# Windowed attention beside dense projections: queries written in place, first token group first, three output tiles moved between later query projections

## The chip, the cores and the metric

The kernel runs on one core of a Trainium2 chip. The metric is device time in microseconds for one execution, as the median of several. One further execution is profiled, and everything read from "the profile" or "the trace" is of that execution. TensorE (PE) multiplies matrices, VectorE (DVE), ScalarE (ACT) and GpSimd (POOL) do elementwise work, and SyncE (SP) issues most of the DMAs. Each engine works through its own instructions in the order in which they were written; an instruction that waits holds up everything behind it on that engine.

## The reference: what is computed

Two transformer-like layers run on 1024 prompt tokens and 32 sample tokens (1056 together), model width 1024. Layer 0 mixes with a matrix-memory recurrence (mLSTM), layer 1 with attention over a window. Each layer ends in a SwiGLU feed-forward part, and each of the four sub-layers is followed by a layer norm over `alpha * x + sublayer(x)`.

The change lies in the attention of layer 1, which the reference computes so:

```
q = x @ w_q                      # 16 query heads of 64
k, v                             # 2 key/value heads of 64, shared by 8 query heads each
s = q k^T / sqrt(64) - slope * |distance|      # own chunk of 64 and the two before it: 192 keys
p = exp(s - max(s, sink)); p = p / (sum(p) + exp(sink - max))
out = (p @ v) @ w_out
x = layer_norm(alpha * x + out)
```

## The kernel before

**Tiling.** Activations lie transposed: 128 features on the partitions, tokens along the free dimension, 8 feature blocks. Tokens are cut in three groups `GRP` of 384, 384 and 288 for projections, and in four quarters of 264 for output projections. Every matrix product is done with each operand split into a high part (rounded to the 32-bit format that TensorE takes at speed) and a low rest: three matmuls per step of 128 rows (`gemm`, lines 404 to 406). A weight unit is 128 x 1024; it is loaded by SP (line 165), and each of its two halves is split by an ACT cast (line 239) and a POOL or DVE subtraction (line 241).

**Order.** The order of instructions on each engine is fixed when the kernel is built. `Weave` interleaves the work: tasks are generators that emit some instructions and then yield a number of "due" microseconds. Each step of `gemm` lets `3 * (max(n, 256) / 2400 + 0.003)` due microseconds pass, where n is the width of the moving operand, and the tasks that have come due emit their instructions there. `wv.drain` emits a task to its end, or up to a condition, without any dense step between. Weight splits are fed in the same way, one half for each 1.7 due microseconds (`FEED_W`), with at most five halves live at a time (`SLOTS`) unless a half has a tile of its own (`W.home`).

**Attention.** `attention` runs 72 items: eight query tiles j (two heads each) times nine blocks of 128 tokens (the ninth holds the 32 sample tokens); b = 0, 1, 2 belong to token group 0, b = 3, 4, 5 to group 1, b = 6, 7, 8 to group 2. An item passes `scores` (matmuls into the PSUM tile `psS`, then a DVE operation that adds the bias and takes the minimum of the negated scores), `soft` (exponential on ACT, reciprocal on DVE, scaling on POOL at lines 1829 and 1833), `turn` (transposes on PE at line 1854, split by ACT and DVE at lines 1858 and 1859), `values` (matmuls, line 1883) and `place` (ACT copy and two DVE additions into the activations, lines 1896 and 1900). Between the stages lies `gap` = `GAP_A` = 0.5: three gaps for an item, 1.5 due microseconds. The list `JG` gives the order of (pair `jp` of query tiles, token group), six items each: (0,0) (1,0) (0,1) (0,2) (1,1) (1,2), then (2,0) to (2,2), then (3,0) to (3,2).

**Queries.** `q_group(j, g)` projects the 128 query features j (two heads) for token group g. The score matmul wants the high part and the low part of one head stacked on the 128 partitions, for two heads in turn. So the result is scaled and split into the tiles `qh` (ACT, line 1659) and `ql` (DVE, line 1660), of which there is one buffer each, and then SP copies halves of 64 partitions into the tile `Q` with DMAs (line 1672): 4 for a group of 384 tokens, 8 for the group of 288, since its last chunk has 32 tokens. `q_made` counts a query tile as ready 4.0 due microseconds later. A query projection is only begun when the attention has scored all but the last group's items before it (`while ast["scored"] < 6 * (i // 2 - 1)`); until then due time passes with no dense work.

**Values, bias, ends.** `VZ` are two tiles of values with one half of the partitions zero; `pad_values` (line 1749) fills them by SP DMAs, three blocks at a time for the first key/value head, all eight at once for the second. `load_bias` loads one of four bias tiles through SP and writes its end columns on POOL (line 1697); three buffers. For b = 0 `scores` first clears one column of `psS` on DVE (line 1797).

**After the attention.** `mixed_parts` splits the mixed activations into operands for the output projection (lines 434 and 435) and reloads the residual. `mixer_out` then runs eight output tiles for each quarter of the tokens; the first quarter starts when token group 0 is placed for all heads, and the rest of the attention is woven into it. Weight units stand in the order in which they are used: twelve loads of `wqb`, then twice eight of `wout_b`.

Of the kernel before, what the change touches and what calls it, by code (L numbers as in the profile page):

```python
# [9 lines left out]
F32 = mybir.dt.float32  # L10
# [19 lines left out]
LC = 64  # L30
WK = 3 * LC
D_FF = 2816
FT = D_FF // P

# [12 lines left out]
GAP_M = (0.6, 1.666, 1.519, 1.5)  # L47
GAP_A = 0.5

# [235 lines left out]
def kernel(ctx: ExitStack, tc: tile.TileContext, A, O):  # L285
# [61 lines left out]

    U_KV, U_QB = [], []
    for _ in range(2):
        U_KV.append([add("wkv", u) for u in range(2)])  # L350
        U_QB.append([add("wqb", u) for u in range(4)])
    U_QB[1] += [add("wqb", u) for u in range(4, 8)]
    U_QB[0] += U_QB[1][4:]
    U_OUT_B = [[add("wout_b", u) for u in range(8)] for _ in range(2)]
    add_ffn(1)
# [876 lines left out]

    def mixer_out(us, li, lx, opening=None, before=None):

        box = [lx]

        def run(g, cols, after):
            if before:
                before(g)
            if g == 3:  # L1240
                lx = box[0]
                lx.sums = ExitStack()
                su = lx.sums.enter_context(pool("sums"))
                bufs = [new(su, f"su{i}", [P, 2, N4])[:] for i in range(2)]
                wv.drain(lx.norms[1])
# [3 lines left out]
            for i, m in enumerate(order):  # L1249
                u = us[g > 0][m]  # L1250
                W.get(u)
                if g < 2:
                    W.split_to(us[g][min(m + 2, KT - 1)])
                ps = psbank()[:, :N4]
                gemm(ps, wcols(u), [(SX[:, 0, k, cols], SX[:, 1, k, cols]) for k in range(KT)])
                z = ACT[:, m, cols]
                nc.vector.scalar_tensor_tensor(z, z, ALPHA, ps, op0=ALU.mult, op1=ALU.add)
# [394 lines left out]
    def q_group(j, g):  # L1652

        t0, n = GRP[g]
        ps = project(U_QB[g > 0][j], g)
        q = Q[j, g] = new(pb, "Q", [P, 2 * 384], F32R, bufs=4)
        h, l = (new(pb, tag, [P, 384], F32R)[:, :n] for tag in ("qh", "ql"))
        sc = -(HD ** -0.5)
        nc.scalar.activation(h, ps, AF.Copy, scale=sc)
        nc.vector.scalar_tensor_tensor(l, ps, sc, h.bitcast(F32), op0=ALU.mult, op1=ALU.subtract)  # L1660

        def place():
            yield 1.0
            for i in range(2):
                own, other = slice(64 * i, 64 * i + 64), slice(64 - 64 * i, 128 - 64 * i)
                for t, src in ((own, h), (other, l)):
                    for a, m in ((0, LC * (n // LC)), (LC * (n // LC), n % LC)):
                        if m:
                            w = min(m, LC)
                            d = q[t, 2 * a : 2 * a + 2 * m].rearrange("p (c h w) -> p c h w", h=2, w=w)  # L1670
                            r = src[own, a : a + m].rearrange("p (c w) -> p c w", w=w)
                            nc.sync.dma_start(d[:, :, i].bitcast(F32), r.bitcast(F32))

        return wv.launch(place())

# [32 lines left out]
    load_bias(1)  # L1708
    load_bias(2)
    load_sample_bias(0)  # L1710
# [11 lines left out]
    for j in range(4):  # L1722
        placing = q_group(j, 0)
        W.done(U_QB[0][j])
# [18 lines left out]

    def pad_values(tiles, g2):

        for i in range(2):
            r = slice(64 * i, 64 * i + 64)
            v = VR[r, tiles, g2].rearrange("p t a d -> p t (a d)")
            nc.sync.dma_start(VZ[i][r, tiles].bitcast(F32), v.bitcast(F32))

    def v_turn(group, pause):
        yield pause
        for c, c0, L, g, off in CH:
            if g == group:
                pt = new(psb, "T", [P, 512], bufs=2)
                nc.tensor.transpose(pt[:L, :P], vT[g][:, off : off + L], ident[:])
                v_parts(c, pt[:L, :P], L)
                if c % 3 == 2:
                    pad_values(slice(c - 2, min(c + 1, 8)), 0)
                ast["v"] = c + 1  # L1760
                yield 0.8

    ast = {"ready": 0, "scored": 0, "placed": 0, "v": 0}
# [8 lines left out]
    def attention(gap):  # L1772
        S, pairs_ = {}, {}

        def parts(b):

            if b == 0:
                return [(0, 130, 64, 0, 1 + P), (1, 258, P, 0, 1 + LC)]
            if b == 8:
                return [(0, 2, P + DEC, SEQ, 1)]  # L1780
            k0 = (b - 1) * P
            return [(0, 2, WK, k0, 1), (1, 2 + WK, WK, k0 + LC, 1)]

        def scores(j, b):
            _, t0, R, g, off = CH[b]
            jp = j // 2
            if (j, b) == (4, 0):
                load_bias(3)
            s = S[j, b] = {}
# [5 lines left out]
            rows = 2 * n  # L1795
            if b == 0:
                nc.vector.memset(ps[:, 194:195], 0.0)
            for c, at, nk, k0, _ in parts(b):
                lhs = q[:, 2 * (off + n * c) : 2 * (off + n * c) + rows]
                for i, k in enumerate((KH[g2], KL[g2])):  # L1800
                    nc.tensor.matmul(ps[:rows, at : at + nk], lhs, k[:, k0 : k0 + nk], start=i == 0, stop=i == 1)  # L1801
            for c, at, nk, _, w in parts(b):
                first = b != 0 and c == 0
                cols = slice(at - first, at + nk + (not first))
                bc = slice(w - first, w + nk + (not first))
                nc.vector.tensor_tensor_reduce(
                    p[:rows, cols], ps[:rows, cols], bias[:rows, j % 2, bc], 1.0, 3e38,
                    op0=ALU.add, op1=ALU.min, accum_out=st[:rows, 0, c : c + 1],
                )
# [4 lines left out]
        def soft(j, b):  # L1814
            s = S[j, b]
            p, st = s["p"], s["st"]
            rows = 2 * DEC if b == 8 else P
            for c, at, nk, _, _ in parts(b):
                first = b != 0 and c == 0
                cols = slice(at - first, at + nk + (not first))  # L1820
                nc.scalar.activation(
                    p[:rows, cols], p[:rows, cols], AF.Exp, bias=st[:rows, 0, c : c + 1], scale=-1.0,
                    accum_out=st[:rows, 1, c : c + 1],
                )
# [5 lines left out]
            else:  # L1830
                for c, at, nk, _, _ in parts(b):
                    w = p[:rows, at : at + nk]
                    nc.gpsimd.tensor_scalar_mul(w, w, st[:rows, 2, c : c + 1])
# [27 lines left out]
        def values(j, b):  # L1861
# [22 lines left out]
            if (j, b) == (3, 7):  # L1884
                pad_values(slice(0, 8), 1)

        def place(j, b):
            _, t0, R, g, off = CH[b]
            ast["placed"] += 1
            if j % 2 == 0:  # L1890
                return
            po = pairs_.pop((j // 2, b))["po"]
            n, nc_ = (DEC, 1) if b == 8 else (LC, 2)
# [23 lines left out]
    for t in spread:  # L1917
        wv.drain(t)
    wv.drain(placing)
    wv.launch(v_turn(0, 0))  # L1920
# [13 lines left out]
    def q_made():  # L1934
        yield 4.0
        ast["ready"] += 1

    for i, (j, g) in enumerate(QG):
        if i < 4:
            continue  # L1940

        while ast["scored"] < 6 * (i // 2 - 1):
            wv.tick(0.25)
        q_group(j, g)
        wv.launch(q_made())
        if g == 2:
            W.done(U_QB[1][j])
        if (j, g) == (7, 0):
            nparts[0] = 0
# [7 lines left out]
            )  # L1957

    def before(g):
        if g == 0:  # L1960
            wv.drain(task, lambda: ast["placed"] >= last_item(7, 0))
        if g < 3:
            parts_made(g)

# [4 lines left out]

    tasks, lx = mixer_out(U_OUT_B, 2, None, finish, before)  # L1970
    ffn(1, 3, tasks, lx, True)
# [132 lines left out]
```

## Time and profile before

| what | value |
|---|---|
| median of 3 runs | 2243.89 us (2242.85 to 2245.75) |
| the profiled execution's own time | 2245.04 us |
| its span, first to last instruction | 2243.3 us |
| PE busy | 2181.9 us (97%) |
| DVE, ACT, POOL busy | 1428.2, 989.4, 933.0 us (64%, 44%, 42%) |
| mean granted TensorE clock | 0.988 |
| PE busy outside 1190 to 1453 us | 1960.1 of 1980.3 us |
| PE busy from 1190 to 1453 us | 221.7 of 263.0 us |

Each line of a timeline names the start, the duration, the engine, the line of the kernel, the operation, what it writes and reads and, in brackets, how long the engine stood idle before it and what ended that. A line of waits gives total, number and longest. The attention begins at about 1216 us with the first score matmuls and its last value matmuls end at about 1453 us. Times that the prediction is made against are those of the profiled execution, 1.15 us above the median.

### The profile page before, as it was taken

What the parts mean: (1) busy time and instruction counts of PE and PEld (TensorE: products, weight loads), DVE (VectorE), ACT (ScalarE), POOL (GpSimd) and SP (SyncE); (2) the same over time, 40 slices, a digit from 0 to 9 for tenths busy, and PEclk for the clock granted to TensorE, in tenths of its full rate; (3) what the DMA queues carried; (4) which work ended last, traced back from release to release, by engine and by line L of the source; (5) the groups of instructions that cost most, each with busy time, mean ns of one, the idle gap of its engine ahead of it and who ended that gap; (6) DMA issues with size and microseconds to landing.
All of it is one profiled execution on the core that took longest, in us unless ns stands there. A gap on an engine that the chain in (4) does not pass through costs nothing.

```text
span 2243.3 us, 43908 instructions
## 1 busy us (share of the span) xinstructions
PE 2181.9 (97%) x16982; PEld 2150.6 (96%) x16982; DVE 1428.2 (64%) x2778; ACT 989.4 (44%) x2215; POOL 933.0 (42%) x920
## 2 busy tenths in 40 slices
PE   9999999999999999999997898899999999999997
PEld 9999999999999999999996888899999999999997
DVE  4465677787756565566575556688766665466657
ACT  4444455364444444322254556756444444431225
POOL 2544210005656555554444433500565556554541
PEclk9999999999999999999998999999999999999999
DMA  5222213213434433996425332421343344398722
GB/s 168 77 61 56 58 38 106 68 38 99 162 134 154 147 141 116 323 303 206 139 86 135 87 78 70 150 87 41 104 173 141 140 151 146 120 339 273 232 67 78
DMA packets 203296, 296.60 MB, mean 132 GB/s; under 512 B 53264, under 2 KB 159560, under 8 KB 203088
## 3 DMA queue, kind: packets, MB, share of 16 engines
q1 hardware_dynamic: 198736, 289.47, 39.5%
q10 hardware_dynamic: 4352, 4.33, 0.6%
q8 instruction: 134, 2.20, 0.4%
q14 instruction: 74, 0.61, 0.1%
HBM read 199.27 MB, written 82.94 MB: 126 GB/s over the span
## 4 chain that ended last, share of the span: by engine, by line
PE 85%; DVE 5%; ACT 3%; DMA 3%; issue 1%; POOL 1%; SPq 1%; ACTq 0%; POOLq 0%; DVEq 0%
PE d L404 10%; PE d L406 10%; PE d L405 10%; PE A L404 9%; PE A L406 9%; PE A L405 9%; PE B L404 7%; PE B L405 7%; PE B L406 7%; PE O L1883 1%; PE psS L1801 1%; PE T L1854 1%; ACT act L507 1%; POOL wl L241 1%; DMA hs_x<-z 1%
## 5 line engine op out<-in xcount | busy, mean ns | idle before, releaser
L241 POOL TENSOR_TENSOR wl_s<-wr,wh_s 128x512 fp32r<-128x512 f32 x224 | 304.3, 1367 | 237.1 <-ACT wh_s L239 163.7
L404 PE MATMUL d<-sx,wh 128*128 128x264 f32 (+2 forms) x1080 | 349.4, 324 | 1.4 <-ACT wh L239 1.3
L406 PE MATMUL d<-sx,wl 128*128 128x264 f32 (+2 forms) x1080 | 331.5, 307 | 2.1 <-POOL wl L241 2.1
L405 PE MATMUL d<-sx,wh 128*128 128x264 f32 (+2 forms) x1080 | 331.6, 307 | 0.2 <-DVE sx L435 0.2
L241 POOL TENSOR_TENSOR wl_a<-wr,wh_a 128x512 fp32r<-128x512 f32 x112 | 153.3, 1371 | 410.7 <-ACT wh_a L239 405.4
L404 PE MATMUL A<-sx,wh_s 128*128 128x264 f32 x896 | 254.4, 284 | 0.0
L405 PE MATMUL A<-sx,wh_s 128*128 128x264 f32 x896 | 254.2, 284 | 0.0
L406 PE MATMUL A<-sx,wl_s 128*128 128x264 f32 x896 | 254.0, 283 | 0.0
L239 ACT CAST wh_s<-wr 128x512 fp32r<-128x512 f32 x224 | 135.7, 618 | 192.3 <-DVE wr L194 102.6
L404 PEld LDWEIGHTS d<-sx,wh 128*128 128x128 f32 x1080 | 206.8, 192 | 5.8 <-ACT wh L239 2.5
L406 PEld LDWEIGHTS d<-sx,wl 128*128 128x128 f32 x1080 | 205.8, 191 | 3.5 <-POOL wl L241 3.2
L405 PEld LDWEIGHTS d<-sx,wh 128*128 128x128 f32 x1080 | 206.9, 192 | 1.8 <-DVE sx L435 0.8
L404 PE MATMUL d<-sx,ex 128*128 128x264 f32 x624 | 180.5, 289 | 0.1
L405 PE MATMUL d<-sx,ex 128*128 128x264 f32 x624 | 177.2, 284 | 0.0
L406 PE MATMUL d<-sx,ex 128*128 128x264 f32 x624 | 176.9, 284 | 0.0
L406 PEld LDWEIGHTS A<-sx,wl_s 128*128 128x128 f32 x896 | 168.8, 188 | 0.0
L405 PEld LDWEIGHTS A<-sx,wh_s 128*128 128x128 f32 x896 | 168.4, 188 | 0.0
L404 PEld LDWEIGHTS A<-sx,wh_s 128*128 128x128 f32 x896 | 168.4, 188 | 0.0
L241 POOL TENSOR_TENSOR wl<-wr,wh 128x512 fp32r<-128x512 f32 (+2 forms) x82 | 106.5, 1304 | 119.1 <-ACT wh L239 109.2
L1325 POOL TENSOR_TENSOR z<-z 128x528 fp32r<-128x528 f32 x76 | 103.4, 1360 | 126.0 <-ACT z L1324 117.1
L404 PE MATMUL A<-ex,wh_s 128*128 128x264 f32 x448 | 127.5, 285 | 0.0
L405 PE MATMUL A<-ex,wh_s 128*128 128x264 f32 x448 | 127.1, 284 | 0.0
(359 smaller groups left out, 7107.0 us busy)
## 6 DMA issues: line engine op xcount, KB each, us to landing
wr<-in_gu SPq DMA_DIRECT2D x92, 512.0 KB, 4.7
hs_x<-z SPq DMA_DIRECT2D x72, 528.0 KB, 3.0
hs_t<-z SPq DMA_DIRECT2D x64, 528.0 KB, 2.9
sx<-hs_x SPq DMA_DIRECT2D x112, 264.0 KB, 5.9
sx<-hs_t SPq DMA_DIRECT2D x64, 264.0 KB, 6.0
ex<-hs_t SPq DMA_DIRECT2D x64, 264.0 KB, 5.9
wr<-in_dn SPq DMA_DIRECT2D x32, 512.0 KB
ex<-hs_x SPq DMA_DIRECT2D x32, 264.0 KB, 5.9
```

Source lines behind the costliest of these rows:

```text
L239: self.nc.scalar.copy(hi, r)
L241: eng.tensor_sub(lo, r, hi.bitcast(F32))
L404: nc.tensor.matmul(out, ah, bh, start=start and k == 0, stop=False, **kw)
L405: nc.tensor.matmul(out, ah, bl, start=False, stop=False, **kw)
L406: nc.tensor.matmul(out, al, bh, start=False, stop=stop and k == last, **kw)
L507: nc.scalar.activation(z, z, AF.Identity, scale=gk, bias=bk)
L1325: eng.tensor_sub(lo.bitcast(F32R), buf(s), hi)
L1801: nc.tensor.matmul(ps[:rows, at : at + nk], lhs, k[:, k0 : k0 + nk], start=i == 0, stop=i == 1)
L1854: nc.tensor.transpose(pt[:nk, t, :rows], p[:rows, at : at + nk], ident[:rows, :rows])
L1883: nc.tensor.matmul(out, v[:nk], x, start=i == 0, stop=i == len(todo) - 1)
```

## The change

- **Queries in place.** `q_group` no longer makes `qh` and `ql` or any DMA. For each of the two heads, ACT writes the scaled high part from PSUM straight into its half of the partitions of `Q`, and DVE writes the low part into the other half. A group of 384 takes two ACT and two DVE instructions of 64 partitions, the group of 288 four of each (256 columns and 32 columns). `q_made` waits 2.5 instead of 4.0 due microseconds.
- **Order.** `JG` becomes (0,0) (1,0) (2,0) (3,0), then for each jp (jp,1) (jp,2). The queries of group 0 get weight loads of their own, so `wqb` is loaded 16 times instead of 12.
- **Output tiles.** After (0,2), (1,2) and (2,2) one output tile of the first quarter is computed (`EARLY` = 3); `mixer_out` skips these three. The second halves of the first quarter's output weights get one tile of their own (`home`), shared by all eight units.
- **Values and ends.** `pad_values` becomes a POOL copy of one block (64 x 128), 28 of them in all. The score layout for b = 0 moves to columns whose end is cleared once, so the clearing in `scores` goes.
- **Bias.** With the new order the four bias tiles are gone through twice; the next is loaded at each visit.
- **Pace.** `GAP_A` goes from 0.5 to 0.46.

```
-GAP_A = 0.5
+GAP_A = 0.46
...
+    for b in (0, 4):
         U_KV.append([add("wkv", u) for u in range(2)])
-        U_QB.append([add("wqb", u) for u in range(4)])
...
+        U_QB[0] += [add("wqb", u) for u in range(b, b + 4)]
+    for jp in range(QH // 4):
+        U_QB[1] += [add("wqb", 2 * jp + i) for i in range(2)]
+        if jp < EARLY:
+            U_OUT_B[0].append(add("wout_b", jp))
...
-        h, l = (new(pb, tag, [P, 384], F32R)[:, :n] for tag in ("qh", "ql"))
...
-        nc.scalar.activation(h, ps, AF.Copy, scale=sc)
-        nc.vector.scalar_tensor_tensor(l, ps, sc, h.bitcast(F32), op0=ALU.mult, op1=ALU.subtract)
...
+        for a, w in ((0, LC), (LC * (n // LC), n % LC)):
+            m = n // LC * LC if w == LC else w
+            if not m:
+                continue
+            src = ps[:, a : a + m].rearrange("p (c w) -> p c w", w=w)
+            dst = q[:, 2 * a : 2 * a + 2 * m].rearrange("p (c h w) -> p c h w", h=2, w=w)
             for i in range(2):
                 own, other = slice(64 * i, 64 * i + 64), slice(64 - 64 * i, 128 - 64 * i)
...
-                            nc.sync.dma_start(d[:, :, i].bitcast(F32), r.bitcast(F32))
...
+                h = dst[own, :, i]
+                nc.scalar.activation(h, src[own], AF.Copy, scale=sc)
+                nc.vector.scalar_tensor_tensor(
+                    dst[other, :, i], src[own], sc, h.bitcast(F32), op0=ALU.mult, op1=ALU.subtract
+                )
...
-    ENDS = (1, 2 * WK + 2)
+    ENDS = (1, 2 * WK + 2, 464)
...
+    home = [new(pb2, "oh", [P, D // 2], F32R, bufs=2)[:] for _ in range(2)]
+    W.home.update({(u, 1): home for u in U_OUT_B[0]})
...
+    def pad_values(i, c, g2):
+
+        r = slice(64 * i, 64 * i + 64)
+        nc.gpsimd.tensor_copy(VZ[i][r, c], VR[r, c, g2].rearrange("p a d -> p (a d)").bitcast(F32))
...
-    JG = [(0, 0), (1, 0), (0, 1), (0, 2), (1, 1), (1, 2)]
-    JG += [(2, 0), (2, 1), (2, 2), (3, 0), (3, 1), (3, 2)]
+    JG = [(jp, 0) for jp in range(4)] + [(jp, g) for jp in range(4) for g in (1, 2)]
...
-            if (j, b) == (4, 0):
-                load_bias(3)
+            if j % 2 == 0 and b in (0, 3):
+                ast["visit"] += 1
+                if ast["visit"] < 7:
+                    load_bias((ast["visit"] + 1) % 4)
...
-            if b == 0:
-                nc.vector.memset(ps[:, 194:195], 0.0)
...
-        yield 4.0
+        yield 2.5
...
+        while ast["scored"] < 6 * (n - 1):
             wv.tick(0.25)
-        q_group(j, g)
...
+        for j in (2 * jp, 2 * jp + 1):
+            q_group(j, g)
+            wv.launch(q_made())
+            if g != 1:
+                W.done(U_QB[g > 0][j])
...
+        if g == 2 and jp < EARLY:
+            before(0)
+            out_tile(U_OUT_B[0][jp], jp, QUARTERS[0][0])
+            W.done(U_OUT_B[0][jp])
```

More of the change, by code (lines that the diff above doesn't have):

```diff
@@ L31 @@
 WK = 3 * LC
+EARLY = 3
 D_FF = 2816
@@ L1231, with out_tile, mixer_out @@
     W.pause = FEED_W
-    def mixer_out(us, li, lx, opening=None, before=None):
+    def out_tile(u, m, cols):
+        ps = psbank()[:, :N4]
+        gemm(ps, wcols(u), [(SX[:, 0, k, cols], SX[:, 1, k, cols]) for k in range(KT)])
+        z = ACT[:, m, cols]
+        nc.vector.scalar_tensor_tensor(z, z, ALPHA, ps, op0=ALU.mult, op1=ALU.add)
+    def mixer_out(us, li, lx, opening=None, before=None, made=0):
         box = [lx]
@@ L1249, in run @@
             for i, m in enumerate(order):
+                if not g and m < made:
+                    continue
                 u = us[g > 0][m]
@@ L1253, in run @@
                     W.split_to(us[g][min(m + 2, KT - 1)])
[L1254 to L1257, printed above, removed]
+                out_tile(u, m, cols)
                 if g == 3 or u not in us[1]:
@@ L1801, in scores @@
                     nc.tensor.matmul(ps[:rows, at : at + nk], lhs, k[:, k0 : k0 + nk], start=i == 0, stop=i == 1)
[L1802 removed]
+            for c, src, at, nk, _, w in parts(b):
                 first = b != 0 and c == 0
                 cols = slice(at - first, at + nk + (not first))
+                sc = slice(src - first, src + nk + (not first))
                 bc = slice(w - first, w + nk + (not first))
                 nc.vector.tensor_tensor_reduce(
[L1807 removed]
+                    p[:rows, cols], ps[:rows, sc], bias[:rows, j % 2, bc], 1.0, 3e38,
                     op0=ALU.add, op1=ALU.min, accum_out=st[:rows, 0, c : c + 1],
@@ L1817, in soft @@
             rows = 2 * DEC if b == 8 else P
-            for c, at, nk, _, _ in parts(b):
+            for c, _, at, nk, _, _ in parts(b):
                 first = b != 0 and c == 0
@@ L1830, in soft @@
             else:
-                for c, at, nk, _, _ in parts(b):
+                for c, _, at, nk, _, _ in parts(b):
                     w = p[:rows, at : at + nk]
@@ L1891, in place @@
                 return
+            if j == 3 and 0 < b < 8:
+                for i in range(2):
+                    pad_values(i, b - i, 1)
             po = pairs_.pop((j // 2, b))["po"]
```

66 lines of the change are left out of this document (22 added, 44 removed).

## The prediction

> **What bounds the kernel now.** I read the sums by stretch first. The columns are the stretch, its length, then busy time and count of PE, PE's weight load, DVE, ACT and POOL, the granted TensorE clock, the DMA share and GB/s.
>
> ```profile
> span 2243.3 us, 43908 instructions
> ...
> 0.00:1190.00 1190.00, 1183.55 (x9175) 1170.12 (x9176) 755.86 (x1470) 508.43 (x1137) 479.47 (x533) 1.00 0.39 128
> 1190.00:1453.00 263.00, 221.73 (x1466) 207.01 (x1465) 151.69 (x590) 157.67 (x500) 114.05 (x131) 0.92 0.36 97
> 1453.00:2243.30 790.30, 776.58 (x6346) 773.44 (x6344) 520.62 (x719) 323.26 (x579) 339.50 (x257) 1.00 0.44 150
> ...
> 1190.00:1200.00 10.00, 7.33 (x31) 5.66 (x30) 8.43 (x12) 5.75 (x11) 5.36 (x4) 0.83 0.66 185
> ...
> 1210.00:1220.00 10.00, 7.89 (x30) 7.26 (x31) 2.58 (x18) 2.50 (x10) 3.46 (x4) 0.67 0.65 163
> 1220.00:1230.00 10.00, 10.00 (x55) 9.43 (x54) 4.64 (x23) 5.48 (x23) 3.16 (x5) 0.74 0.05 11
> ...
> 1270.00:1280.00 10.00, 5.93 (x26) 5.76 (x26) 5.41 (x23) 6.89 (x21) 4.95 (x5) 0.66 0.33 86
> ...
> 1360.00:1370.00 10.00, 6.50 (x31) 6.28 (x32) 5.73 (x23) 7.50 (x24) 4.91 (x5) 0.66 0.28 78
> ...
> 1453.00:1464.00 11.00, 11.00 (x93) 11.00 (x92) 7.83 (x17) 6.01 (x12) 1.29 (x1) 1.00 0.67 204
> ```
>
> Outside the attention PE idles 20 us in 1980. In the attention it idles 41.3 of 263 us, and the clock is 0.92 instead of 1. All that the change can win is there: 41.3 us, and at most 221.73 x 0.08 = 17.7 us of clock, together 59. Next, what PE waited for in that stretch (total, times, longest), and the four long waits in the timeline.
>
> ```profile
> PE T L1854 <- POOL s L1829: 15.7, 7, 5.3
> PE T L1756 <- DVE VR L1686: 9.7, 1, 9.7
> PE psS L1801 <- DVE psS L1797: 7.3, 8, 1.3
> ...
> PE psS L1801 <- DMA Q<-ql: 1.1, 2, 0.8
> ```
>
> ```profile
> 1210.50 0.47 PE L1756 MATMUL T<-ident,act 128*128 128x128 f32 x1 [9.67 <-DVE VR L1686]
> ...
> 1274.07 0.90 PE L1854 MATMUL T<-ident,s 128*128 128x128 f32 x3 [5.30 <-POOL s L1829]
> ...
> 1310.60 0.90 PE L1854 MATMUL T<-ident,s 128*128 128x128 f32 x3 [3.68 <-POOL s L1829]
> ...
> 1363.51 0.90 PE L1854 MATMUL T<-ident,s 128*128 128x128 f32 x3 [4.75 <-POOL s L1829]
> ```
>
> DVE and POOL are named, but they were themselves late. The last view, ACT's timeline just ahead of each, and the queries' tile among SP's issues, show why.
>
> ```profile
> 1200.70 0.49 ACT L1659 ACTIVATE qh<-d 128x384 fp32r<-128x384 f32 x1 [2.19 <-DMA Q<-qh]
> 1201.09 1.13 ACT L239 CAST wh<-wr 128x512 fp32r<-128x512 f32 x2
> ...
> 1208.76 0.49 ACT L1659 ACTIVATE qh<-d 128x384 fp32r<-128x384 f32 x1 [6.54 <-DMA Q<-qh]
> ...
> 1270.97 0.41 ACT L1659 ACTIVATE qh<-d 128x288 fp32r<-128x288 f32 x1 [4.17 <-DMA Q<-qh]
> ...
> 1307.65 0.41 ACT L1659 ACTIVATE qh<-d 128x288 fp32r<-128x288 f32 x1 [1.98 <-DMA Q<-qh]
> ...
> 1360.60 0.41 ACT L1659 ACTIVATE qh<-d 128x288 fp32r<-128x288 f32 x1 [4.46 <-DMA Q<-qh]
> ```
>
> ```profile
> L1672 SPq DMA_DIRECT2D Q<-qh x64: 590/605/1699, 1185.0 to 1426.0; - x64
> ```
>
> There is one `qh`. ACT can't write the next until SP's copies of the last have been read; they are 64 from `qh` and as many from `ql`, at 0.6 us of SP each, so a pair of 288-token projections takes 16 x 0.6 = 9.6 us of SP. Behind the blocked ACT instruction stand the exponentials, so POOL's scaling and PE's transposes are late too. So the long waits come from SP's copies, not from the attention's own arithmetic.
>
> **The change part by part.** *The queries' DMAs go.* The three later waits, 5.30 + 3.68 + 4.75 = 13.7 us, each fall in a g = 2 group, where two projections pass 2 x 8 x 0.369 = 5.9 due us and six items need 9.0, so that nothing dense was left to cover. With ACT free the transposes would still wait for their chain; but (0,2), (1,2) and (2,2) are exactly where an output tile now stands, 24 matmuls at 11.00 / 93 = 0.118 us = 2.8 us. I take all 13.7. At 1200 ACT would go on 2.19 us earlier, less 0.49 for the second query instruction: the casts of row 1201.09 come 1.7 us earlier, then POOL's subtraction and the third value transpose, about 1202.5 in place of 1210.5. Of 9.67 I take 7.8. The 1.1 us on `Q<-ql` goes. Sum 22.6.
>
> *The clearing of psS goes.* The 7.3 us are eight waits for a 0.06 us memset behind DVE's queue. The scores then wait for the bias operation two items earlier, still on DVE. Bounds 0 and 7.3; I take 6, since that operation stands further ahead in the queue.
>
> *The clock.* Work lost to it is busy time x (1 - clock): 7.33 x 0.17 + 7.89 x 0.33 + 10.00 x 0.26 = 6.4 us at 1190 to 1230, 5.93 x 0.34 = 2.0 at 1270, 6.50 x 0.34 = 2.2 at 1360: 10.6 next to three of the stalls. Bounds 0 and 17.7 (all of it); I take 9.
>
> *What queries in place add.* Rows by shape, with count, busy time, mean ns, idle before:
>
> ```profile
> L1660 DVE SCALAR_TENSOR_TENSOR ql<-d,qh 128x384 fp32r<-128x384 f32 x15 | 8.3, 554 | 11.7 <-ACT qh L1659 9.1 <-ACT wh L239 2.6
> L1660 DVE SCALAR_TENSOR_TENSOR ql<-d,qh 128x288 fp32r<-128x288 f32 x8 | 3.7, 458 | 20.7 <-ACT s L1821 8.7 <-DMA Q<-ql 6.8 <-ACT hi L1858 2.9
> ...
> L1900 DVE TENSOR_TENSOR act<-O,t 64x256 f32<-64x256 f32 x64 | 26.6, 415 | 5.7 <-ACT t L1896 4.5 <-PE psS L1801 0.4
> ...
> L1618 DVE TENSOR_TENSOR KL<-d,KH 128x256 fp32r<-128x256 f32 x1 | 0.4, 415 | 0.0
> ...
> L1618 DVE TENSOR_TENSOR KL<-d,KH 128x32 fp32r<-128x32 f32 x1 | 0.2, 192 | 0.3 <-ACT KH L1617 0.3
> ```
>
> ```profile
> L1659 ACT ACTIVATE qh<-d 128x384 fp32r<-128x384 f32 x15 | 7.3, 487 | 12.7 <-DMA Q<-qh 10.7 <-PE d L406 1.9
> L1659 ACT ACTIVATE qh<-d 128x288 fp32r<-128x288 f32 x8 | 3.3, 412 | 18.3 <-DMA Q<-qh 13.1 <-PE T L1854 3.2 <-PE d L406 2.0
> ...
> L1617 ACT CAST KH<-d 128x256 fp32r<-128x256 f32 x1 | 0.4, 377 | 0.0
> ...
> L1617 ACT CAST KH<-d 128x32 fp32r<-128x32 f32 x1 | 0.2, 186 | 0.7 <-DVE KL L1618 0.7
> ```
>
> Half the partitions don't halve the time (64x256 at line 1900 takes 415 ns, as 128x256 at line 1618 does). So a 384 group adds one more instruction to each engine, 0.49 and 0.55 us. The 288 group becomes two of 256 and two of 32: ACT 2 x (0.377 + 0.186) - 0.412 = 0.71, DVE 2 x (0.415 + 0.192) - 0.458 = 0.76. Over 16 and 8 groups ACT gains 13.5 us and DVE 14.9. With the eight casts of the four more weights (0.6 us each, by row 1201.09) ACT then has 158 + 18 and DVE 152 + 15 us in a stage of some 235, where PE has 263 - 41.3 - 17.7 = 204 of full-speed work: PE's matmuls hide both. Without that cover all 33 us would be on the path (0 to 33). The short waits of today (15.7 less 13.7 us on POOL's scaling) say that the queues are seldom late; I charge 3.
>
> The page "VectorE: DVE Perf Modes" of the Trainium skill, section "Two Vector instructions with no wait between them", speaks against this part: an instruction whose input or output starts in another quarter of the partitions than its predecessor's starts only when all earlier ones have finished, and the new low parts read one half and write the other. Line 1900, which also writes both halves in turn, shows no longer duration for it. What a held start can cost is the overlap of neighbours:
>
> ```profile
> 1194.15 0.41 DVE L505 TENSOR_SCALAR act<-act,lng,lnb 128x264 f32<-128x264 f32 x1
> 1194.48 0.69 DVE L499 TENSOR_TENSOR act<-act,z 128x528 f32<-128x528 f32 x1
> ```
>
> By that rule 64 new instructions, each late itself and making its successor late by this overlap of 0.08 us, add 10 us to DVE, which is still less busy than PE; the sum stays.
>
> *POOL.* The four more query weights are eight halves, and there are 28 value copies:
>
> ```profile
> L241 POOL TENSOR_TENSOR wl<-wr,wh 128x512 fp32r<-128x512 f32 x36 | 47.2, 1315 | 37.8 <-ACT wh L239 33.7 <-issue 2.4 <-DMA scrx<-act 1.3
> ...
> L1833 POOL TENSOR_SCALAR s<-s,st 128x128 f32<-128x128 f32 x8 | 4.8, 606 | 0.0
> ...
> L1697 POOL COPY bt<-nsink 64x2 f32<-64x2 f32 x4 | 0.6, 186 | 0.0
> ```
>
> Halves: 8 x 1.3 = 10.5 us. No row shows a copy of 64x128: it lies between 0.19 (64x2) and 0.61 (a scaling of 128x128); I take 0.3, nearer the copy, 8 us in all (5 to 17). Six more bias loads in this stretch, four copies each, make 4.5. POOL goes from 114 to about 137 us of 230. The copies wait for DVE's value parts, later for the value matmuls; behind them stand POOL's scalings, and PE's transposes wait for those. I charge 2 (0 to 23).
>
> *Three tiles moved, one tile of their own for the second halves.* The matmuls are the same. The first moved tile waits for the last two splits of group 0: 1 us (0 to 3). Of the five left, four can have their second half cast only when the tile before has ended: one ACT cast, then 1.3 us on POOL, 2 us with half a tile of matmuls, 1.4 us, and some attention in front: 2 us in all (0 to 8). At the end the attention has three tiles, 8.5 us, less cover: after the last queries 8 items are left to score and two follow through, 10 x 1.38 = 13.8 due us against 5 x 2.71 = 13.6. Just enough; 2 us (0 to 8.5). In front of the attention no dense work is lost.
>
> *The sum.* 22.6 + 6 + 9 = 37.6 us won, 3 + 2 + 1 + 2 + 2 = 10 us lost: 27.6, say 28. 2245.0 - 28 = 2217 for a profiled execution; the median lies 1.15 us lower: **2216**.
>
> **The rivals.** *All of it, and the waits that are left too.* With steady dense work the short idles and the slow clock go as well: 22.6 + 7.3 + 17.7 = 47.6 with hardly any cost: 2196. For it: the order now balances dense and attention time in every group (8.3 due us for six items; 7.8 for two projections of 384, 5.9 + 2.7 for two of 288 and a tile). Against: three engines get more work.
>
> *The place of the waits is taken.* ACT and DVE, fuller, are late at each query group; if half of the added 28 us of query instructions comes on the path and the clock is won back by half only, 22.6 + 3 + 4.5 - 14 - 5 = 11: 2233. For it: ACT is at 7.50 of 10 in the stretch at 1360 although it was blocked there for 4.46. Against: that was the jam after the block.
>
> *Slower: the end of the attention stands bare.* If the attention lags, so that the last items run with no dense matmuls, each costs its chain. From the release at 1360.60 to the transpose at 1363.51 are 2.9 us for one item, whose own PE work is some 1.3 (204 us less 108 of dense work, 15 groups of 384, 10 of 288 and 5.5 tiles at 0.118 us for 264 columns, over 72 items): 1.6 us idle, and as much again at half clock, 3 us. Over the gain of 37.6 less the other costs of 8 it decides from ten such items on; twelve (two groups) give 2245.0 - 29.6 + 36 = 2251, 2250 as a median. For it: cover is moved forward and the order leaves (3,1) and (3,2) for the last. Against: the pace of 0.46 leaves just enough due time, and the splits of group 0 are out of the way by then.
>
> *It doesn't do what it says:* ACT writes to `Q` wait for the score matmuls that read its buffer (four buffers), so that the block stays in another form: within 0.2% of 2244. Against: the items that read it are scored a whole projection earlier.
>
> The Trainium skill's page "SBUF — State Buffer", section "SBUF: two separate sides", has a rule that favours the second rival: POOL and DVE share a pair of ports that one instruction holds to its end. No row here isolates it; a POOL subtraction takes 1.3 us in the mean here.
>
> **How the numbers follow.** Chances: forecast 0.58 (2206 to 2227), all of it 0.14, place taken 0.14, no effect 0.04, slower 0.10. The range is 2194 to 2238: left out above are slower (0.10), no effect (0.04) and a little of the second rival (0.02), below a little of the first (0.04). I call faster what is over 0.2% (4.5 us) below, which is about what a measurement can tell: 0.58 + 0.14 + 0.13 = 0.85; within 0.2% 0.06; slower 0.09.
>
> **What would show it.** Right: no `Q` DMA, no ACT wait for one, PE idle between 1190 us and the last value matmul under 20 us, granted clock there above 0.96, no wait on a memset. Wrong: idle on POOL's scaling well above 2 us outside the old places (ACT, DVE or POOL too full); PE waits for line 241 in the last five tiles (the shared tile); a row of long idles after the last query projection (bare end).

## The result, and the profile after

The changed kernel takes 2232.96 us (median of 4 runs, 2231.79 to 2233.75) beside 2244.36 us of the kernel before: a ratio of 0.9949, 95% interval 0.9932 to 0.9966. The gain is 11.4 us, where 28 were forecast. 2233 lies inside the range of 2194 to 2238 and outside the forecast's own 2206 to 2227. It is the time that the second rival ("the place of the waits is taken") was given.

The profiled execution took 2232.42 us. Its span divides into PE busy and PE idle as follows; a lower clock shows as longer busy time for the same matmuls.

| | span | PE busy | PE idle | mean granted clock |
|---|---|---|---|---|
| before | 2243.3 | 2181.9 | 61.4 | 0.988 |
| after | 2230.6 | 2176.4 | 54.2 | 0.994 |

So 7.2 us of idle and 5.5 us of slow clock are gone. The sums by stretch of the kernel after, columns as in the prediction:

```profile
span 2230.6 us, 43755 instructions
...
0.00:1190.00 1190.00, 1183.57 (x9181) 1170.80 (x9181) 756.80 (x1471) 509.18 (x1139) 478.20 (x529) 1.00 0.39 128
1190.00:1443.90 253.90, 222.77 (x1516) 205.78 (x1515) 168.58 (x626) 175.35 (x547) 136.02 (x192) 0.96 0.26 78
1453.00:2230.60 777.60, 763.79 (x6241) 760.71 (x6239) 510.40 (x699) 316.07 (x565) 338.40 (x256) 1.00 0.43 149
```

From 1190 us to the last value matmuls at 1443.9 PE still idles 253.90 - 222.77 = 31.1 us, where the prediction wanted under 20, and the clock there is 0.96. What PE waited for from 1185 to 1460 us (total, times, longest):

```profile
PE T L1861 <- POOL s L1836: 9.7, 12, 2.0
PE O L1890 <- DVE act L1908: 6.4, 4, 1.8
PE T L1762 <- DVE VR L1692: 5.1, 1, 5.1
PE d L408 <- ACT wh L240: 4.0, 1, 4.0
PE d L410 <- DVE wl L242: 2.8, 1, 2.8
```

The wait on a memset is gone, and none names a DMA. The long waits on POOL's scaling (5.30, 4.75, 3.68) have become twelve short ones, and new rows stand beside them. The cause is in the same view for ACT, 1180 to 1453 us:

```profile
ACT Q L1677 <- DVE Q L1678: 29.5, 40, 2.6
ACT hi L1865 <- DVE lo L1866: 13.4, 16, 1.8
```

Before, ACT stood 23.8 us blocked on the query DMAs, 8 times. Now it stands 29.5 us blocked on DVE, 40 times, in the very instructions that replaced them: ACT's high part of the second piece waits for DVE's low part of the first. Forty is the number of such hand-overs: one in each of 16 groups of 384 tokens, three in each of 8 groups of 288. The chain of work that ended last shows one group of 288 (start, duration, what; the short pieces of issue are left out):

```profile
1290.41 0.43 DVE Q L1678
...
1290.86 0.39 ACT Q L1677
...
1291.28 0.44 DVE Q L1678
...
1291.73 0.20 ACT Q L1677
...
1291.96 0.20 DVE Q L1678
...
1292.18 0.19 ACT Q L1677
...
1292.39 0.62 ACT wh L240
```

The two engines take turns. ACT's first piece was written at 1289.20; the fourth ends at 1292.37, 3.17 us later, although the four need 0.38 + 0.38 + 0.19 + 0.19 = 1.14 us. Behind them stand the weight cast, the copy `t`, then DVE's additions and PE's value matmuls, which start at 1294.52 after 1.82 us of idle.

### The profile page after: what moved, and what is told of

Its sections match the earlier page's. It is cut to its first block, busy times and chain, and to the rows that moved or that the text cites. A ratio compares the mean times of both kernels' runs of the same rounds, so it can differ in the third digit from the quotient of the medians.

```text
span 2230.6 us, 43755 instructions
## 1 busy us (share of the span) xinstructions
PE 2176.4 (98%) x16982; PEld 2143.3 (96%) x16982; DVE 1444.7 (65%) x2812; ACT 1006.7 (45%) x2263; POOL 952.6 (43%) x976
## 3 DMA queue, kind: packets, MB, share of 16 engines
q1 hardware_dynamic: 161632, 282.84, 37.9%
## 4 chain that ended last, share of the span: by engine, by line
PE 83%; DVE 8%; ACT 5%; DMA 2%; issue 1%; POOL 1%; SPq 0%; ACTq 0%; DVEq 0%; POOLq 0%
PE d L408 9%; PE A L408 9%; PE d L410 9%; PE A L410 9%; PE A L409 9%; PE d L409 9%; PE B L408 7%; PE B L409 7%; PE B L410 7%; PE O L1890 1%; ACT s L1828 1%; ACT act L511 1%; DVE Q L1678 1%; DMA hs_x<-z 1%; DMA sx<-hs_t 1%
## 5 line engine op out<-in xcount | busy, mean ns | idle before, releaser
L408 PE MATMUL d<-sx,wh 128*128 128x264 f32 (+2 forms) x1048 | 338.4, 323 | 4.1 <-ACT wh L240 4.0
L410 PE MATMUL d<-sx,wl 128*128 128x264 f32 (+2 forms) x1048 | 321.6, 307 | 4.2 <-DVE wl L242 2.8
L409 PE MATMUL d<-sx,wh 128*128 128x264 f32 (+2 forms) x1048 | 321.3, 307 | 0.4 <-DVE sx L439 0.4
L408 PEld LDWEIGHTS d<-sx,wh 128*128 128x128 f32 x1048 | 199.5, 190 | 7.4 <-ACT wh L240 4.3
L410 PEld LDWEIGHTS d<-sx,wl 128*128 128x128 f32 x1048 | 198.8, 190 | 5.5 <-DVE wl L242 3.3
L409 PEld LDWEIGHTS d<-sx,wh 128*128 128x128 f32 x1048 | 199.8, 191 | 1.5 <-DVE sx L439 0.7
```

Source lines behind the costliest of these rows:

```text
L408: nc.tensor.matmul(out, ah, bh, start=start and k == 0, stop=False, **kw)
L409: nc.tensor.matmul(out, ah, bl, start=False, stop=False, **kw)
L410: nc.tensor.matmul(out, al, bh, start=False, stop=stop and k == last, **kw)
```

## The experiments

**Theory and rivals.** The theory: the order in which ACT and DVE take turns on one projection holds up ACT. Rivals: the engines are simply too full with the added instructions; the three early tiles, the shared tile, POOL's copies or the pace of 0.46 cost more than forecast.

**All high parts first** (the change, with this edit in `q_group`). The instructions are the same; only their order differs.

```
+        todo = []
...
-                h = dst[own, :, i]
-                nc.scalar.activation(h, src[own], AF.Copy, scale=sc)
-                nc.vector.scalar_tensor_tensor(...)
+                todo.append((dst[own, :, i], dst[other, :, i], src[own]))
+        for h, l, s in todo:
+            nc.scalar.activation(h, s, AF.Copy, scale=sc)
+        for h, l, s in todo:
+            nc.vector.scalar_tensor_tensor(l, s, sc, h.bitcast(F32), ...)
```

> The changed kernel with one edit: at each query group all high parts (ACT) are written before all low parts (DVE), where the change takes them in turn, head by head. Theory A (the alternation is the new wait: ACT's second high part stands behind DVE's first low part, 29.5 us of ACT idle in 40 waits): that wait falls under 3 us, PE idle from 1185 us to the end of the attention falls by some 8 us, time 2224. Theory B (ACT, DVE and POOL are simply fuller, the order of the pieces is nothing): 2233 as the changed kernel. Theory C (the pace of 0.46 is too tight): 2233.

**The queries in place alone** (the kernel before with only the new `q_group`; one kernel in the order of the change, one with the high parts first).

> The kernel before with only the queries written in place, in the change's own alternating order; order of groups, pace, output tiles, value copies, clearing and due time of 4.0 as before. Theory A: the three waits of 13.7 us at the g = 2 groups lose ACT's block on DMA but get the alternation in its place; 2236. Theory B: as the instructions are the same, 2234, most of the gain of the change. If the gain of the change came from the new order and the output tiles instead, 2242.

> The same as the in-place queries alone, with all high parts ahead of all low parts. Theory A: 8 us under the alternating one, 2228. Theory B: no difference between the two.

**The pace** (the change with `GAP_A = 0.5`).

> The changed kernel with the attention's gap back at 0.5. Theory C (the tighter gap makes PE wait for POOL's scaling, 9.7 us in 12 waits): those waits fall by half and the time to 2228. Theory A and B: 2233 within 2 us; rather a little slower, since at 0.5 the three tiles moved leave a barer end (10 x 1.5 = 15.0 due us against 13.6).

These four ran beside the same runs of the kernel before (2245.75 us):

| kernel | us | ratio, 95% interval |
|---|---|---|
| change, pace 0.5 | 2232.71 | 0.9937 [0.9915, 0.9959] |
| change, high parts first | 2215.19 | 0.9857 [0.9831, 0.9883] |
| before + queries in place, taking turns | 2245.62 | 0.9997 [0.9987, 1.0008] |
| before + queries in place, high parts first | 2230.02 | 0.9925 [0.9903, 0.9947] |

With the same instructions in another order the change takes 2215.2 us, 17.8 us less than it does, and within 1 us of what was forecast for the change. The effect of the order was expected, but only about half as large (9 and 8 us). Queries in place alone, taking turns, are worth nothing at all, which none of the three expectations (2234 to 2242) had; with the high parts first they are worth 15.7 us. ACT's waits in the changed kernel with the high parts first, and PE's:

```profile
ACT hi L1866 <- PE T L1862: 18.0, 26, 2.8
ACT hi L1866 <- DVE lo L1867: 14.2, 16, 1.8
```

```profile
PE T L1862 <- POOL s L1837: 3.6, 6, 1.1
PE T L1862 <- POOL s L1841: 3.4, 4, 1.7
...
PE d L410 <- DVE wl L242: 2.7, 1, 2.7
PE O L1891 <- DVE act L1909: 2.3, 2, 1.7
...
PE T L1763 <- DVE VR L1693: 1.6, 1, 1.6
```

The row of ACT's `Q` waiting for DVE's `Q` is gone, and PE's idle time over the whole span falls from 54.2 to 40.8 us. ACT and DVE are as busy as in the change over the whole span (1007.0 and 1443.6 us beside 1006.7 and 1444.7), so fullness was not the cause. The pace is not it either: 2232.71 with 0.5 beside 2232.96 with 0.46 (the second measured beside another set of runs of the kernel before), and with the high parts first 0.5 again makes no difference:

> The changed kernel with the high parts first (2215), and the attention's gap at 0.5 instead of 0.46. In the alternating kernel the gap made no difference (2232.7 against 2233.0). If the gap of 0.46 pays once ACT is free, 2218; if not, within 2 us of 2215.

It took 2214.39 us, 0.986 [0.9843, 0.9876].

**What makes ACT wait.** Two things could tie ACT's second piece to DVE's first: both engines use the same `Q` (DVE reads the high part from it and writes the low part into it), or both read one projection tile `d` in PSUM. Two kernels test this and keep the order in turns. The first (the kernel before with queries in place) takes DVE's writes to `Q` away: the low parts go to tiles of their own, and POOL copies them into `Q`. DVE still reads the high part from `Q`.

```
+        lows = []
...
-                nc.vector.scalar_tensor_tensor(dst[other, :, i], src[own], sc, ...)
+                low = new(pb, f"low{i}", [P, 384], F32R, bufs=2)[other, :m]...
+                nc.vector.scalar_tensor_tensor(low, src[own], sc, ...)
+                lows.append((dst[other, :, i], low))
+        for d, s in lows:
+            nc.gpsimd.tensor_copy(d, s.bitcast(F32))
```

> The kernel before with the queries in place in the alternating order, but DVE's low parts go to tiles of their own and POOL copies them into the query tile afterwards. It settles what orders the alternation. If it is the query tile (DVE's low part and ACT's next high part are both written to it), ACT's wait on DVE in the query row (29.2 us in 39 waits in the version without the copies) falls under 5 us. If it is the projection's PSUM tile, which ACT and DVE both read, the wait stays at 20 to 30 us.

The wait stayed (ACT's waits; DVE's line writes `low` now). A single run took 2250.44 us beside 2247.06.

```profile
ACT Q L1668 <- DVE low L1670: 30.2, 39, 2.6
```

The second (the change) lets ACT alone read PSUM: one more ACT instruction copies the scaled projection to an SBUF tile `qf`, and DVE takes the low parts from there.

```
+        full = new(pb, "qf", [P, 384], bufs=1)[:, :n]
+        nc.scalar.activation(full, ps, AF.Copy, scale=sc)
...
+            alt = full[:, a : a + m].rearrange("p (c w) -> p c w", w=w)
...
-                nc.vector.scalar_tensor_tensor(dst[other, :, i], src[own], sc, ...)
+                nc.vector.tensor_sub(dst[other, :, i], alt[own], h.bitcast(F32))
```

> The changed kernel in its alternating order, but ACT first copies the scaled projection once from PSUM into a tile in SBUF, and DVE takes the low parts from that copy, so that only ACT reads the PSUM tile. ACT has 24 more instructions, some 11 us. If the order comes from the PSUM tile that both engines read, ACT's wait on DVE in the query row falls from 29.5 us to under 5, and the time to about 2220. If it comes from the query tile, to which both write and which DVE reads, the wait stays above 20 us and the time is 2233 or more.

It took 2215.92 us, 0.9867 [0.9849, 0.9884]. ACT's waits, and then two groups by shape (count, busy, mean ns, idle before):

```profile
ACT hi L1866 <- DVE lo L1867: 13.3, 16, 1.8
ACT hi L1866 <- PE T L1862: 11.0, 19, 1.3
```

```profile
L1669 ACT ACTIVATE qf<-d 128x384 f32<-128x384 f32 x16 | 7.9, 492 | 5.8 <-PE d L410 4.4 <-DVE Q L1681 1.3
L1680 ACT ACTIVATE Q<-d 64x384 fp32r<-64x384 f32 x32 | 15.4, 481 | 0.4
```

The wait between the pieces is gone, 0.4 us over 32 instructions, though the order still takes turns, and DVE still reads from `Q` and writes to it. So `Q` is not what ties the two engines; it is the shared reading of one PSUM tile that is put in order. And although ACT has 24 instructions more (7.9 us for those of 384 alone), the kernel is 17 us faster than the change, and about as fast as the one with the high parts first (0.9867 beside 0.9857; the intervals overlap). Fullness of ACT costs little here.

**Clearing once** (before with queries in place, high parts first; and the column layout of the change, so that `scores` doesn't clear).

```
-    ENDS = (1, 2 * WK + 2)
+    ENDS = (1, 2 * WK + 2, 464)
...
-            if b == 0:
-                nc.vector.memset(ps[:, 194:195], 0.0)
```

> In-place queries alone with the high parts first (2230), and besides only the clearing of the score tile once at the start, with the new columns for block 0. The prediction put 6 of 7.3 us on it. If that holds, the waits on the memset (8.8 us in 8 waits) go and the time is 2223. Rival: the scores then wait for the bias operation of two items before instead, and the time stays within 2 us of 2230.

2219.11 us, 0.9872 [0.9856, 0.9889]; without this edit 0.9925 [0.9903, 0.9947]. The difference, 0.0053 of 2245 us, is 12 us, known to some 6 us either way by the two intervals. PE's waits without the edit, then with it:

```profile
PE T L1851 <- POOL s L1826: 13.0, 9, 2.5
PE psS L1798 <- DVE psS L1794: 8.8, 8, 1.8
```

```profile
PE T L1850 <- POOL s L1825: 13.5, 11, 2.5
PE d L404 <- ACT wh L239: 3.0, 2, 1.7
```

Eight waits of together 8.8 us go, with no row in their place; PE idles 7.4 us less in the span (52.5 to 45.1) and is busy 4.8 us less (2176.2 to 2171.4), which is clock.

**The other parts, taken out of the changed kernel with the high parts first** (2215.19 us, 0.9857): the shared tile for second halves (`W.home.update` removed), the three early tiles (`EARLY = 0`), POOL's value copies (SP DMAs of the same blocks in their place).

> The changed kernel with the high parts first (2215), and the second halves of the first quarter's output weights in the common slots again, with no tile of their own. If the shared tile costs 2 us at the last tiles as the prediction had it, 2213. If it is what frees slots for the query weights, PE waits on weight casts come up and the time is 2218 or more.

> The changed kernel with the high parts first (2215), and no output tile moved forward: all eight after the last query projection. If the tiles are what covers the g = 2 groups (three times some 3 us of matmuls), PE waits of 2 to 4 us on POOL's scaling come back near three of these groups and the time is 2222. If with ACT free no cover is needed there, the time is 2212, for the end of the attention has 8.5 us more cover.

> The changed kernel with the high parts first (2215), and the 28 value copies as SP DMAs of one block each instead of POOL copies. The copies took 289 ns each on POOL, 8 us in all, beside the prediction's charge of 2 us for POOL. If POOL's fuller queue costs that, 2213; if it costs nothing, 2215; if 28 more DMAs hold up the value matmuls, 2218 and PE waits on them appear.

| without | us | ratio, 95% interval |
|---|---|---|
| the shared tile | 2211.44 | 0.9839 [0.9824, 0.9854] |
| the early tiles | 2219.26 | 0.9873 [0.9858, 0.9888] |
| POOL's copies | 2213.11 | 0.9856 [0.9841, 0.9871] |

The copies cost no more than 28 DMAs in their place (the ratio is the same), though each takes 289 ns (8.1 us in all, in the kernel after):

```profile
L1755 POOL CAST VZ<-VR 64x128 fp32r<-64x128 f32 x28 | 8.1, 289 | 1.1
```

The shared tile and the early tiles shift the time by some 4 us each, one up, one down. The intervals overlap that of the kernel that they are compared with, so these two sizes are likely, not settled. Without the shared tile the 2.7 us on `DVE wl` (in PE's rows of the kernel with the high parts first) are no longer among PE's waits, but other waits are longer: PE idles 41.9 us in the span, beside 40.8 with the tile. What falls is its busy time, from 2172.3 to 2167.8 us, which is clock. The 20 us around that wait, with the shared tile and then without it (columns as in the sums by stretch):

```profile
1420.00:1440.00 20.00, 17.02 (x107) 15.94 (x108) 16.84 (x37) 10.62 (x25) 0.68 (x1) 0.83 0.61 201
```

```profile
1420.00:1440.00 20.00, 18.47 (x141) 17.34 (x140) 17.90 (x41) 11.22 (x28) 0.68 (x1) 1.00 0.68 225
```

The granted clock there is 0.83 with the tile and 1.00 without it: 17.02 x 0.17 = 2.9 of the 4.5 us.

Without the early tiles PE idles 2.9 us more (43.7). It isn't POOL's scaling that grows much, as had been expected, but the value matmuls' wait for the placing of an earlier result (PE's waits):

```profile
PE O L1891 <- DVE act L1909: 5.0, 6, 2.4
PE T L1862 <- POOL s L1837: 4.7, 7, 1.1
```

**A version that beats both.** The same taking of turns stands in `turn`: for the first and last block the transposed weights are split piece by piece, and ACT's second `hi` waits for DVE's first `lo` (13.4 us in 16 in the kernel after). This kernel has the high parts first there too, and no shared tile; a second one has the pace at 0.43 besides.

```
             for t, nk in cuts:
                 nc.scalar.copy(hi[:nk, t, :rows], pt[:nk, t, :rows])
+            for t, nk in cuts:
                 nc.vector.tensor_sub(lo[:nk, t, :rows], ...)
...
-    W.home.update({(u, 1): home for u in U_OUT_B[0]})
```

> High parts first and no tile of their own for the second halves (2211), and besides, in the transposes of blocks 0 and 8, both ACT copies ahead of both DVE subtractions. There ACT waits 13.8 us in 16 times on DVE, by the same order on a PSUM tile. If each such wait costs PE what the ones in the query groups did (29.5 us of ACT for 18 us of time), 2203. If blocks 0 and 8, with half the score work of the others, have slack enough, 2210.

> As the one before, with the gap at 0.43. If the attention now runs ahead of the dense work, it lengthens the stretch with nothing but dense matmuls at the end and shortens no wait: within 2 us of it. If it leaves more cover at the end, 2 us less.

The first takes **2207.31 us**, 0.9829 [0.9815, 0.9844], 37 us less than the kernel before and 26 less than the change. With 0.43 it is 2210.78 us, 0.9843 [0.9828, 0.9858]: no gain. In the first, no wait of `hi` on `lo` is left among ACT's waits. Beside the kernel without the shared tile (2211.44 us, 0.9839) this is 4 us by the medians and 2 us by the ratios; PE idles 37.9 us in the span beside 41.9. The two intervals overlap, so that part is likely, not settled.

## Why the prediction was right and wrong

**What bounds the kernel: right.** One `qh`, ACT blocked by SP's copies, all behind it late. The whole gain lies in the attention, in idle and clock, as was said: before 1190 and behind 1453 us PE still idles 6.4 + 13.8 = 20.2 us in the kernel after, as in the one before.

**The step that failed: what queries in place add.** The prediction counted the new instructions, laid them beside PE's 204 us of work and charged 3 us. The counts and durations hold (64x384: 486 ns on ACT, 555 on DVE, beside 487 and 554 before with 128 partitions). What it didn't ask is what the second ACT instruction of a group waits for. In the old order there was one instruction of ACT and one of DVE for a tile; the new order hands one PSUM tile back and forth, and that took the place of the DMA block: 29.5 us of ACT's time instead of 23.8, and 17.8 us of the kernel's.

The trace of before had it. Two rows that the prediction quoted for their durations end in `0.7 <-DVE KL L1618 0.7` and `0.3 <-ACT KH L1617 0.3`: keys, where ACT's second piece of one tile `d` waited for DVE's reading of the first. And in ACT's waits from 1190 to 1453 us the pattern stands two lines below the block on the DMAs:

```profile
ACT qh L1659 <- DMA Q<-qh: 23.8, 8, 6.5
...
ACT hi L1858 <- DVE lo L1859: 7.2, 16, 0.9
```

That is the same pattern on another PSUM tile: 16 hand-overs, 0.45 us each. For the 40 new ones an estimate from this row is 40 x 0.45 = 18 us of ACT waits. They are 29.5, in part at least because a hand-over also waits for whatever DVE has ahead. The longest of all shows that, in ACT's timeline and then in DVE's:

```profile
1189.71 0.48 ACT L1677 ACTIVATE Q<-d 64x384 fp32r<-64x384 f32 x1
1192.83 0.49 ACT L1677 ACTIVATE Q<-d 64x384 fp32r<-64x384 f32 x1 [2.63 <-DVE Q L1678]
1193.34 0.62 ACT L240 CAST wh<-wr 128x512 fp32r<-128x512 f32 x1
```

```profile
1190.12 1.35 DVE L497 SCALAR_TENSOR_TENSOR z<-z 128x264 f32<-128x264 f32 x1
1191.50 0.71 DVE L503 TENSOR_TENSOR act<-act,z 128x528 f32<-128x528 f32 x1
1192.24 0.55 DVE L1678 SCALAR_TENSOR_TENSOR Q<-d,Q 64x384 fp32r<-64x384 f32 x1
```

Two operations of the layer norm stood in DVE's queue ahead of the low part, and the weight cast waited behind ACT's second piece. With the high parts first the two pieces follow one another and the cast starts at 1191.07 instead of 1193.34:

```profile
1190.08 0.97 ACT L1679 ACTIVATE Q<-d 64x384 fp32r<-64x384 f32 x2
1191.07 0.62 ACT L240 CAST wh<-wr 128x512 fp32r<-128x512 f32 x1
```

Whether the chip needs this wait is another matter. The Trainium skill's page "PSUM — Partial Sum Buffer", section "PSUM bank collisions raise a hardware error", says that two engines may not touch the same bank in the same quarter of the partitions at once, reads included, and that different quarters of one bank may be touched together; it calls a guard by whole bank the simple version. The pieces of two heads lie in different halves of the partitions, so by that page the guard by quarter would let them overlap. No run here has such an overlap: it wasn't tried. What the runs show is the price of a wait for the whole tile, and that one order of the instructions doesn't pay it.

**The other terms.**

| term | predicted, us | runs |
|---|---|---|
| DMA block gone | 22.6, clock apart | the DMA waits are gone; in the old order with the high parts first 15.7 with its clock, 8.9 of it idle (nothing in turns) |
| clearing gone | 6, clock apart | 12, of it 7.4 idle, the rest clock |
| clock | 9 | busy time 5.5 less in the change, 9.6 with the high parts first (2181.9 to 2172.3) |
| added instructions | -3 | -17.8, by their order alone |
| POOL's copies and halves | -2 | copies: no more than DMAs in their place; halves not tried apart |
| first moved tile late | -1 | not tried apart |
| shared tile | -2 | about -4, as clock and not as waits |
| end of the attention | -2 | no row of long idles; not tried apart |

*The block on DMA.* In the old order, with the DMAs gone and the high parts first, 13.0 us of waits on POOL's scaling remain; of 15.7 us before, 13.7 were to vanish. The rest was won by the new order and the tiles together (3.6 us on line 1837 remain there). At the start the third value transpose was to come 7.8 us earlier. Before it came at 1210.5 us; it comes at 1207.0 in the change, where ACT stands in two more hand-overs ahead of the value parts (1.13 and 0.62 us), and at 1205.2 with the high parts first. So 22.6 was too much: for the whole change with its order mended the same three items make 12.1 (15.7 less 3.6 on POOL's scaling) + 5.3 (1210.5 less 1205.2 at the start) + 1.1 (the wait on a DMA) = 18.5 us.

*The clearing* was probably the second size that was off. It was bounded above by its idle time of 7.3 us; PE's busy time fell besides by 4.8 us, the mean granted clock rising from 0.992 to 0.995, and clock had been counted only next to the long stalls.

*The later start of the low parts*, weighed as 10 us of DVE and nothing on the path, is there, and it is not the step that failed. In the kernel before, the low part could begin while the operation ahead of it still ran; now it begins 0.03 us after that one's end, some 0.1 us later each time. DVE's timeline, two lines of before and then two of after:

```profile
1322.64 0.08 DVE L1806 DVE_READ_ACCUMULATOR2_ANT st<- 128x1 f32 x1
1322.64 0.55 DVE L1660 SCALAR_TENSOR_TENSOR ql<-d,qh 128x384 fp32r<-128x384 f32 x1
```

```profile
1290.30 0.08 DVE L1813 DVE_READ_ACCUMULATOR2_ANT st<- 128x1 f32 x1
1290.41 0.42 DVE L1678 SCALAR_TENSOR_TENSOR Q<-d,Q 64x256 fp32r<-64x256 f32 x1
```

The kernel with the high parts first has it too (1285.48 behind a 0.08 us operation that started at 1285.36) and is 17.8 us faster all the same.

*POOL's copies* took 289 ns, as the 0.3 us that was taken. But a row of the kernel before did show a copy of 64x128, outside the attention:

```profile
L920 POOL COPY qz<-qT 64x128 f32<-64x128 f32 x64 | 19.2, 299 | 1.8
```

*The shared tile* was to cost waits at the last five tiles. There is none on its halves there. The wait that goes with it comes once, after the attention (2.7 to 2.8 us for a low half that DVE splits at line 242), and what is won without the tile is clock.

*The early tiles* are worth some 4 us, though only to a small part (4.7 beside 3.6 us) by covering POOL's scaling at the end of a group, as was argued.

*The rivals.* The second one was priced right, 2233, and for its main sign (idle on POOL's scaling well above 2 us outside the old places: 9.7 us in 12) it would have been believed. But its reason, fuller engines, is refuted by the second kernel of the PSUM pair: more ACT work and 17 us less time. So its price was right by luck. "The end stands bare" fell: with the high parts first PE is busy for all 20 us from 1440 to 1460. The first rival's 2196 was not reached; the best kernel still idles 37.9 us in the span. That the change with its reads in order takes 2215.2 us, the forecast's 2216, is in part luck: the clearing was put too low and the DMAs too high.

## What to carry to other kernels

When a transfer is replaced by instructions of two engines that read one PSUM tile, count not only instructions but hand-overs, and let one engine take all its pieces before the other begins: here that order alone decided between 0 and 15.7 us, and between 11 and some 30. A row of the trace that is quoted for its duration should be read to its end: "what ended the idle time before" showed the pattern at another place. And a tiny instruction that the matmuls wait for on a busy queue costs its wait and clock besides: some 12 us here for eight clearings of 0.06 us.

## What the runs showed of the hardware

Half the partitions took the same time as all of them on both engines (64x384: 486 and 555 ns; 128x384: 487 and 554 ns). A DVE operation got three times as long beside a POOL subtraction; DVE's timeline of the kernel after, then POOL's:

```profile
1194.56 1.36 DVE L509 TENSOR_SCALAR act<-act,lng,lnb 128x264 f32<-128x264 f32 x1
1196.46 0.40 DVE L509 TENSOR_SCALAR act<-act,lng,lnb 128x264 f32<-128x264 f32 x1
1198.36 1.39 DVE L509 TENSOR_SCALAR act<-act,lng,lnb 128x264 f32<-128x264 f32 x1
```

```profile
1194.03 1.74 POOL L242 TENSOR_TENSOR wl<-wr,wh 128x512 fp32r<-128x512 f32 x1 [2.85 <-ACT wh L240]
1198.30 1.29 POOL L242 TENSOR_TENSOR wl<-wr,wh 128x512 fp32r<-128x512 f32 x1 [2.53 <-ACT wh L240]
```

The one that starts while POOL is idle takes 0.40 us, the two that overlap a subtraction 1.36 and 1.39 and end about when it does. This agrees with the rule of the Trainium skill's page "SBUF — State Buffer", section "SBUF: two separate sides", that POOL and DVE share ports which one instruction holds to its end, for which the prediction had no row. What it is worth in this kernel was not measured.
